# A hybrid decoder layer on one core: fewer hand-overs inside the samples' attention, two background tasks issued later, another warm-up

## The chip, the cores and the metric

The kernel runs on one core of a Trainium2 chip. The core has five engines that work side by side, each through its own queue in order: TensorE (PE, matrix products; the loading of its weights is shown apart as PEld), VectorE (DVE), ScalarE (ACT), GpSimd (POOL) and SyncE (SP), which here only issues transfers. Matrix products read SBUF and write PSUM, eight banks of 128 partitions x 512 floats. Transfers from HBM run on 16 shared DMA engines, whichever queue issued them.

The metric is the device time of one launch, in microseconds (us). Before the change the median of three runs is 2834.9 us (2831.94 to 2835.55).

## The reference, cut to what matters

One decoder layer is computed for two groups that share all weights: a prompt of 256 tokens and 8 samples of 8 new tokens each, with 2048 tokens in the past. That gives 320 columns in all.

```python
x = layer_norm(ALPHA * x + 0.5 * swiglu(x, ffn1_w_up, ffn1_w_down))        # 2048 -> 2 x 5632 -> 2048
rq, rk, rv, rg, nq, nkv, ng = split(x @ w_in)                              # one input projection
ro = silu(rg) * group_norm(retention(rope(rq), rope(rk), rv, state))       # 4 heads
# NSA, 8 query heads, 2 KV heads, three branches:
kc, vc = compress(k_cmp), compress(v_cmp)                                  # blocks of 32 keys, stride 16
p_cmp  = softmax(q @ kc);  o_cmp = p_cmp @ vc
idx    = top_k(p_cmp @ cover, 16)                                          # 16 blocks of 64 keys
o_slc  = softmax(q @ k_slc[idx]) @ v_slc[idx]
o_win  = softmax(q @ k_win) @ v_win                                        # last 512 keys
no     = g0 * o_cmp + g1 * o_slc + g2 * o_win
x = layer_norm(ALPHA * x + concat(ro, no) @ w_out)
x = layer_norm(ALPHA * x + 0.5 * swiglu(x, ffn2_w_up, ffn2_w_down))        # then the outputs
```

All arithmetic is float32 in name. The kernel splits each weight and each activation into a high and a low part of a shorter float format (`fp32r`) and adds three products: high x high, high x low, low x high (`mm3`, L213 to L217).

## The kernel before

**Main products.** All weight matrices are cut into chunks of 512 KB (256 rows x 512 columns) which pass in one fixed order through four raw buffers, three split buffers and four PSUM banks `m0` to `m3`. A chunk is loaded by an SP transfer (`w_load`, L269), split by ACT (high part, L221) and DVE (low part, L222), and used in 4 x 6 = 24 products of 128x128 weights by 320 columns (`sweep`, L301). `w_feed` (L275) issues splits and loads at each new chunk; a load waits on the SP queue until the split of the chunk that held its raw buffer is done.

**Background tasks.** Everything else (compression, selection, the samples' attention, the prompt's attention, retention, the norms' small work) is written as Python generators, and the program's order is fixed when it is built, by a planner. The planner has a clock, the sum of the nominal PE times of all products issued so far. After every six main products, nominally 0.816 us, `main` calls `tick` (L231), which advances up to two tasks that are due. A task says with `yield t` that it wants to go on t us of the planner's clock later, and with `yield condition` that it waits for a condition. A `yield 0.0` also ends the task's step: it goes on at the next tick at the earliest, after six more main products. `until` (L248) advances tasks without main products until a condition holds. The clock is an estimate; on the chip every engine follows the fixed order and waits by semaphores.

**Samples' attention** (`sample`, L1289). It takes four groups of two samples, one after the other. Each group reads ten tiles: the window keys (`wkt`), four tiles of paged keys (`pks`, 8 transfers of 128 KB each on SP, after two loads of page numbers), the window values (`cwin`), four tiles of paged values (`pvs`, two gathers each on POOL, L1223). The tiles share a ring of slots: two at first, four once the selection of all groups is done (`a_count == 4`), three after `r1` is taken away (L1480). `feed` (L1299) keeps the ring full less one and estimates when each tile arrives: 2.5 us after the issue or the previous tile's estimate, whichever is later, plus 4.5 us for paged keys and 3.0 us for others. `arrival()` is what is left of that estimate, zero if it is past. Keys: scores of one tile (`coltile`, eight PE records), then 0.7 us later scaling and the block mask on DVE, then the next tile. Values: `turn(c)` transposes four pieces of the probabilities on PE (L1377) and copies them out on DVE or ACT; `values(c)` multiplies them with the tile (32 PE records). Tile c's `values` comes after `turn(c+1)`.

**Selection** (`select`, L1229). For each of the four groups: scores of compressed keys, softmax, scaling by the reciprocal (L1247, DVE), a pause of 1.5, transposition (L1250, PE), then ranking of 30 blocks by five DVE passes over 900 elements. After group g it sets `a_count = g + 1`. `sample` starts group g when `a_count > g`. After the fourth, `v_natural` (L1103) transposes the prompt's values in three steps and then sets `vn_done`, for which `prompt` (L1543) waits; `mix` (L1516) waits for the last sample group and the last prompt head and starts retention. The evacuation of the retention queries (L1447) runs tasks until `a_count == 4`, and the second half of the output projection (L1938) runs tasks until retention is done.

**Prompt's compression** (`prompt_compress`, L1124). Sixteen weight tiles of 512 KB (`cw1k`, `cw1v`) pass through two halves of a buffer. The first two are loaded at the start of the task; each of the others is issued on SP when the tile two places before it is used. The products start 7.0 us after the task begins, one tile every 2.8 us. `pc_done` at its end is awaited by `select`.

**Start** (L322). While the first inputs come in, PE multiplies a matrix of constants by itself 11 times (float32, 128 columns, L347; each product leaves two records) into a bank that is not read.

Of the kernel before, what the change touches and what calls it, by code (L numbers as in the profile page):

```python
# [9 lines left out]
F32R = mybir.dt.float32r  # L10
# [13 lines left out]
SCALE = 128.0 ** -0.5  # L24
PAST = 2048

WARM = 11
NTMP = 5


# [139 lines left out]
class Builder:  # L170
# [38 lines left out]
    def mm(self, out, lhsT, rhs, start, stop, us):  # L209
        self.nc.tensor.matmul(out, lhsT, rhs, start=start, stop=stop)  # L210
        self.clock += us
# [110 lines left out]
    def start(self):  # L322

        self.x_rings = [self.sb.ring(4 * KT * NT, name=f"x{k}") for k in range(2)]

        self.kh, self.kl = 0, 1
        self.xh, self.xl = ([self.x_room(k, [128, NT], F32R) for _ in range(KT)] for k in range(2))
        raw = [self.t([128, 6, NT], f"G{5 + i}") for i in range(3)]
        self.xraw = [raw[q // 3][:, 2 * (q % 3):2 * (q % 3) + 2] for q in range(8)]
        for q in range(8):  # L330
            if q:
                self.nc.sync.dma_start(out=self.xraw[q], in_=self.I["xT"][:, 2 * q:2 * q + 2, :])
            else:

                r, w = self.raw[:, 0], self.wq[0]
                self.nc.sync.dma_start(out=self.xraw[0], in_=self.I["xT"][:, 0:2, :])
                for k in range(2):
                    self.nc.sync.dma_start(out=r[:, 512 * k:512 * k + 512], in_=w[:, 512 * k:512 * k + 512])
                self.raws[0], self.n_dma = r, 1
            if 0 < q < 4:  # L340
                self.w_load()

        self.ones = self.t([128, 128], "ones")
        self.nc.vector.memset(self.ones, 1.0 / 256.0)
        ps = self.p("m3")
        for _ in range(WARM):
            self.nc.tensor.matmul(ps[:, 0:128], self.ones, self.ones, start=True, stop=True)  # L347
        hi, lo = (self.t([128, 1024], t, F32R) for t in ("wh0", "wl0"))
        r = self.raws.pop(0)
        for k in range(2):  # L350
            c = slice(512 * k, 512 * k + 512)
            self.split(self.xh[k], self.xl[k], self.xraw[0][:, k])
            self.split(hi[:, c], lo[:, c], r[:, c])
        self.halves[0] = hi, lo
        self.n_split = 1
        self.x_split(1)
        self.w_split()
# [766 lines left out]
    def prompt_compress(self):  # L1124
        nc = self.nc
        wk = self.vn[:, 1536:1920]
        stage = self.t([128, 2, 1024], "G6")

        def load(n):
            raw = stage[:, n % 2]  # L1130
            nc.sync.dma_start(out=raw, in_=self.I["cw1" + "kv"[n // 8]][n % 8])
            return raw

        raws = [load(0), load(1)]
        yield 7.0
        for kind in range(2):
            ph = yield from self.hold()
            for i in range(8):
                raw = raws.pop(0)
                for s2 in range(2):  # L1140
                    s = 2 * i + s2
                    for r in range(2):
                        j = (2 * s + r) % 4
                        o = (s2 * 2 + r) * 256

                        at = 640 * kind + 16 * r + s
                        self.mm(ph[32 * j:32 * j + 32, 0:256], self.kvt[:, at:at + 497:16],
                                raw[:, o:o + 256], s < 2, s >= 14, 0.127)
                if 8 * kind + i < 14:
                    raws.append(load(8 * kind + i + 2))  # L1150
                yield 2.8
            h4 = wk[:, 0:256]
            nc.scalar.activation(h4, ph[:, 0:256], AF.Copy)
            self.drop(ph)
            yield 1.0
            pf = yield from self.hold()
            for f in range(2):
                self.mm(pf[:, 32 * f:32 * f + 32], h4[:, 128 * f:128 * f + 128], self.k_sum4, True, True, 0.43)
            hs, u = wk[:, 256:320], wk[:, 320:384]
            for f in range(2):  # L1160
                pc = self.posc[:, 2 * kind + f:2 * kind + f + 1]
                nc.scalar.activation(hs[:, 32 * f:32 * f + 32], pf[:, 32 * f:32 * f + 32], AF.Identity, bias=pc)
                nc.scalar.activation(u[:, 32 * f:32 * f + 32], pf[:, 32 * f:32 * f + 32], AF.Square, bias=pc)
            self.drop(pf)
            yield from self.gelu(hs, u)
            yield 3.0
            po = yield from self.hold()
            w2 = self.cw2[kind]
            if kind == 0:
                for f in range(2):  # L1170
                    self.mm(po[:, 0:32], w2[:, f], u[:, 32 * f:32 * f + 32], f == 0, f == 1, 0.43)
                for v in range(2):
                    nc.scalar.activation(self.kcp(v), po[:, 0:32], AF.Copy, scale=0.5)
            else:
                for f in range(2):
                    self.mm(po[0:32, 0:128], u[:, 32 * f:32 * f + 32], w2[:, f], f == 0, f == 1, 0.22)
                nc.scalar.activation(self.vcp[0:32], po[0:32, 0:128], AF.Copy, scale=0.5)
            self.drop(po)
            yield 1.0
        self.pc_done = True  # L1180
# [48 lines left out]
    def select(self):  # L1229
# [7 lines left out]
        for g in range(4):  # L1237
# [7 lines left out]
            self.drop(px)  # L1245
            yield from self.softmax(s, sc, None, (0.8, 0.8))
            nc.vector.tensor_scalar(s, s, sc[:, 0:1], None, op0=ALU.mult)  # L1247
            yield 1.5
            px = yield from self.hold()
            nc.tensor.transpose(px[:, :128], s, self.ident)  # L1250
            self.clock += 0.11
# [37 lines left out]
    def sample(self):  # L1289
# [9 lines left out]
        def feed():  # L1299
            while len(kvq) < len(self.ring) - 1 and order:  # L1300
                g, i = order.pop(0)
                self.kv_time = max(self.kv_time, self.clock + 2.5) + (4.5 if 0 < i < 5 else 3.0)
                kvq.append((self.kv_load(g, i), self.kv_time))

        def arrival():
            return max(0.0, kvq[0][1] - self.clock)

        def take():
            self.kv_tags.pop(0)
            return kvq.pop(0)[0]  # L1310
# [4 lines left out]
        for g in range(4):  # L1315
# [5 lines left out]
            pnn, o = ptr[:, 1536:1664], ptr[:, 1664:1792]  # L1321
# [14 lines left out]
            def new_rows(keys, dst):  # L1336
                pn = yield from self.hold()
                self.coltile(pn, slice(0, 16), q, lambda b, v: keys(v)[:, gs], True, True, 0.07)
                add(dst, pn[:, 0:16], SCALE, self.k_mn, op0=ALU.mult, op1=ALU.add)
                self.drop(pn)  # L1340


            for c in range(4):
                yield arrival()
                kt = take()
                px = yield from self.hold()
                self.coltile(px, slice(0, 512), q, lambda b, v: kt[:, b, :, 128 * v:128 * v + 128], True, True, 0.234)
                feed()
                if c == 1 and g:
                    yield from new_rows(self.kw, sw[:, 512:528])  # L1350
                if c == 2 and g:
                    yield from self.softmax(sw[:, :528], scw, self.grow[:, g, 2:3], (0.8, 0.8))
                yield 0.7
                add(s[:, 512 * c:512 * c + 512].rearrange("p (k r) -> p k r", r=64),
                    px.rearrange("p (k r) -> p k r", r=64), SCALE,
                    self.bm[:, g, 8 * c:8 * c + 8].rearrange("p (k o) -> p k o", o=1).broadcast_to([128, 8, 64]),
                    op0=ALU.mult, op1=ALU.add)
                self.drop(px)
# [28 lines left out]
            def values(c, vt):  # L1387
                n, pt = 1 if c == 5 else 4, pts.pop(c)
                at = 128 * ((c + 3) // 4)
                for k in range(n):  # L1390
                    rhs = (lambda b, v: self.vnew[:, v]) if c == 5 else (lambda b, v: vt[:, b, k, 128 * v:128 * v + 128])
                    self.coltile(po, slice(at, at + 128), lambda j: pt[:, 128 * k + 32 * j:128 * k + 32 * j + 32],
                                 rhs, c in (0, 1, 5) and k == 0, c in (0, 4, 5) and k == n - 1, 0.081)
# [4 lines left out]
            nc.gpsimd.memset(pnn, 0.0)  # L1398
            nc.gpsimd.tensor_scalar(pnn[:, 16 * g:16 * g + 16], s[:, 2048:2064], scs[:, 0:1], None, op0=ALU.mult)
            nc.gpsimd.tensor_scalar(pnn[:, 64 + 16 * g:80 + 16 * g], sw[:, 512:528], scw[:, 0:1], None, op0=ALU.mult)  # L1400
            yield 1.0
            yield arrival()
            values(0, take())
            feed()
            yield 3.5
# [1 line left out]
            yield 1.2  # L1407
            for c in range(1, 5):
                yield from turn(c + 1)
                yield arrival()  # L1410
                values(c, take())
                feed()
                if c < 4:
                    yield 1.8
# [564 lines left out]
```

## Time and profile before

| | |
|---|---|
| median of 3 runs | 2834.9 us |
| the profiled execution, its own time | 2837.03 us |
| its span, first to last instruction | 2835.4 us |
| mean granted TensorE clock | 0.994 |
| PE busy | 2778.3 us, 98% |
| DVE, ACT, POOL busy | 1553.6, 1212.1, 335.4 us |
| HBM read, written | 467.47 MB, 22.28 MB |

Times below are us from the span's start. PE's idle time is the difference between a stretch's length and PE's busy time in it. "Waits" list who waited for whom: us in total, times, longest. A timeline row gives start, length, engine, line, operation, output tile and input tiles, with the idle time before it and what ended it in brackets. `m` tiles are main products, `x` tiles are products of background tasks. "PEclk" is the granted share of the TensorE clock.

### The profile page before, as it was taken

Reading aid. Unit: us, or ns where it says so; the run is one execution under the profiler, and the core shown is the slowest. Engines: PE = TensorE matmul, PEld = TensorE weight load, DVE = VectorE, ACT = ScalarE, POOL = GpSimd, SP = SyncE. Lnnn points to the kernel's source line nnn. Section 1 sums busy time; section 2 is a strip of 40 time slices with the busy share of each in tenths; the row PEclk is TensorE's granted clock in tenths of the full one; section 3 lists DMA queues with packets and bytes.
Section 4 is the critical chain, followed back from the end, with each engine's and each line's share of the span. In section 5 each row is a group of like instructions: output and inputs, shape, how many; then the busy total and the mean of one; then the engine's idle time right before and its main releaser. Section 6 shows DMA issues by size and latency. Waiting matters only on the chain. (4 is left out here: it accounts for less than half of the span.)

```text
span 2835.4 us, 49605 instructions
## 1 busy us (share of the span) xinstructions
PE 2778.3 (98%) x19839; PEld 2704.3 (95%) x19839; DVE 1553.6 (55%) x1933; ACT 1212.1 (43%) x1677; POOL 335.4 (12%) x398
## 2 busy tenths in 40 slices
PE   9999999999999999999999999999999999999997
PEld 9999999999999989998888888999999999999997
DVE  4333333347867769783574455674333333367665
ACT  4333333345445546554444445353333333354554
POOL 0000000000113223213232111330000000001110
PEclk9999999999999999999999999999999999999999
DMA  6555444455656445447667764545444444444442
GB/s 230 182 192 181 149 149 149 151 161 193 202 169 227 144 137 157 141 138 254 200 235 236 234 212 161 207 140 165 150 149 149 150 150 152 151 143 148 150 150 101
DMA packets 201594, 484.75 MB, mean 171 GB/s; under 512 B 24146, under 2 KB 98771, under 8 KB 199443
## 3 DMA queue, kind: packets, MB, share of 16 engines
q1 hardware_dynamic: 191538, 451.30, 49.9%
q0 software_dynamic: 9824, 30.29, 3.1%
q8 instruction: 155, 2.54, 0.4%
q14 instruction: 77, 0.62, 0.1%
HBM read 467.47 MB, written 22.28 MB: 173 GB/s over the span
## 5 line engine op out<-in xcount | busy, mean ns | idle before, releaser
L222 DVE TENSOR_TENSOR wl<-raw,wh 128x1024 fp32r<-128x1024 f32 (+1 forms) x651 | 815.6, 1253 | 1067.3 <-ACT wh L221 1054.5
L221 ACT ACTIVATE wh<-raw 128x1024 fp32r<-128x1024 f32 (+1 forms) x651 | 688.1, 1058 | 1164.8 <-PE m L216 1125.8
L215 PE MATMUL m<-x,wh 128*128 128x320 f32 x3664 | 1144.4, 312 | 3.3 <-ACT x L617 1.5
L216 PE MATMUL m<-x,wh 128*128 128x320 f32 x3664 | 1128.5, 308 | 1.7 <-DVE x L597 1.0
L217 PE MATMUL m<-x,wl 128*128 128x320 f32 x3664 | 1128.5, 308 | 0.2 <-DVE wl L222 0.2
L215 PEld LDWEIGHTS m<-x,wh 128*128 128x128 f32 x3664 | 688.1, 188 | 26.7 <-issue 22.2
L216 PEld LDWEIGHTS m<-x,wh 128*128 128x128 f32 x3664 | 688.4, 188 | 2.8 <-DVE x L597 1.3
L217 PEld LDWEIGHTS m<-x,wl 128*128 128x128 f32 x3664 | 687.7, 188 | 0.8 <-DVE wl L222 0.7
L215 PE MATMUL m<-r,wh 128*128 128x320 f32 (+1 forms) x1592 | 495.2, 311 | 4.0 <-ACT r L221 2.3
L216 PE MATMUL m<-r,wh 128*128 128x320 f32 (+1 forms) x1592 | 488.2, 307 | 4.4 <-DVE r L222 4.4
L217 PE MATMUL m<-r,wl 128*128 128x320 f32 (+1 forms) x1592 | 490.8, 308 | 0.0
L215 PEld LDWEIGHTS m<-r,wh 128*128 128x128 f32 x1592 | 298.9, 188 | 9.9 <-issue 3.7
L216 PEld LDWEIGHTS m<-r,wh 128*128 128x128 f32 x1592 | 299.6, 188 | 6.6 <-DVE r L222 5.8
L217 PEld LDWEIGHTS m<-r,wl 128*128 128x128 f32 x1592 | 298.3, 187 | 0.0
L518 POOL TENSOR_TENSOR t<-x 128x320 f32<-128x320 f32 x3 | 2.8, 919 | 1418.5 <-DVE x L498 716.6
L222 DVE TENSOR_TENSOR r<-G,r 128x640 fp32r<-128x640 f32 (+1 forms) x184 | 155.5, 849 | 0.0
L215 PE MATMUL x<-r,G 128*128 128x256 f32 x480 | 137.6, 287 | 0.0
L216 PE MATMUL x<-r,G 128*128 128x256 f32 x480 | 135.7, 283 | 0.0
L217 PE MATMUL x<-r,G 128*128 128x256 f32 x480 | 135.1, 282 | 0.0
L221 ACT ACTIVATE r<-G 128x640 fp32r<-128x640 f32 (+1 forms) x184 | 130.1, 712 | 0.0
L222 DVE TENSOR_TENSOR r<-x,r 128x512 fp32r<-128x512 f32 (+1 forms) x76 | 79.5, 1053 | 35.9 <-ACT r L221 34.6
L215 PEld LDWEIGHTS x<-r,G 128*128 128x128 f32 x480 | 91.8, 191 | 1.0 <-issue 1.0
(394 smaller groups left out, 2233.1 us busy)
## 6 DMA issues: line engine op xcount, KB each, us to landing
raw<-wup SPq DMA_DIRECT2D x351, 512.0 KB, 3.5
raw<-wdn SPq DMA_DIRECT2D x176, 512.0 KB, 3.6
raw<-win_ret SPq DMA_DIRECT2D x48, 512.0 KB, 4.3
raw<-win_nsa SPq DMA_DIRECT2D x40, 512.0 KB, 3.8
raw<-wout SPq DMA_DIRECT2D x32, 512.0 KB, 3.7
r<-pks SPq DMA_DIRECT2D x96, 128.0 KB, 3.5
x<-pkc SPq DMA_DIRECT2D x152, 64.0 KB, 2.3
K<-cw1k SPq DMA_DIRECT2D x16, 512.0 KB, 4.5
```

The lines of the kernel that those rows point to most:

```text
L215: mm(out, wh, xh, start=start, stop=False)
L216: mm(out, wh, xl, start=False, stop=False)
L217: mm(out, wl, xh, start=False, stop=stop)
L221: self.nc.scalar.activation(hi, src, AF.Copy)
L222: self.nc.vector.tensor_tensor(lo, src, hi.bitcast(F32), op=ALU.subtract)
L518: nc.gpsimd.tensor_tensor(s, self.d[0], self.d[1], op=ALU.add)
```

## The change

Five edits of the planned order, none of the computation:

- the warm-up is 24 products of an `fp32r` copy of the constants, 160 columns each, with two alternating 128-column weights, instead of 11 float32 products; a DVE copy of 128x512 makes their operand first
- the prompt's compression starts its products 9.0 instead of 7.0 after its first loads
- the selection's transposes come 2.8 instead of 1.5 after the scaling
- before a paged key tile, and before the value tiles 1 to 4, the task hands over only if `arrival()` is not zero; a zero no longer ends the step
- before value tile 0 the two pauses, 1.0 and then `arrival()`, become one pause of the larger of the two, taken at the earlier moment

The `yield arrival()` before the window keys (L1325) stays.

```diff
-WARM = 11
+WARM = 24
...
-        for _ in range(WARM):
-            self.nc.tensor.matmul(ps[:, 0:128], self.ones, self.ones, start=True, stop=True)
+        warm = self.t([128, 1024], "wh2", F32R)[:, 0:512]
+        self.nc.vector.tensor_copy(warm.rearrange("p (k c) -> p k c", k=4),
+                                   self.ones.rearrange("p (o c) -> p o c", o=1).broadcast_to([128, 4, 128]))
+        for k in range(WARM):
+            self.nc.tensor.matmul(ps[:, 0:160], warm[:, 128 * (k % 2):128 * (k % 2) + 128], warm[:, 256:416], start=True, stop=True)
...
         raws = [load(0), load(1)]
-        yield 7.0
+        yield 9.0
...
             nc.vector.tensor_scalar(s, s, sc[:, 0:1], None, op0=ALU.mult)
-            yield 1.5
+            yield 2.8
             px = yield from self.hold()
             nc.tensor.transpose(px[:, :128], s, self.ident)
...
             for c in range(4):
-                yield arrival()
+                if arrival():
+                    yield arrival()
                 kt = take()
...
-            yield 1.0
-            yield arrival()
+            yield max(1.0, arrival())
             values(0, take())
...
             for c in range(1, 5):
                 yield from turn(c + 1)
-                yield arrival()
+                if arrival():
+                    yield arrival()
                 values(c, take())
```

## The prediction

> **What bounds the kernel now.** First the page, then PE's time by stretches, then PE's waits.
>
> ```profile
> span 2835.4 us, 49605 instructions
> PE 2778.3 (98%) x19839; PEld 2704.3 (95%) x19839; DVE 1553.6 (55%) x1933; ACT 1212.1 (43%) x1677; POOL 335.4 (12%) x398
> 10.40:20.00 9.60, 9.60 (x66) 9.60 (x67) 5.96 (x9) 6.20 (x12) 0.00 (x0) 1.00 0.99 392
> 1310.00:1380.00 70.00, 70.00 (x517) 62.92 (x515) 26.35 (x35) 29.83 (x52) 19.97 (x33) 1.00 0.66 217
> sum 420.00, PE 405.50 PEld 356.87 DVE 224.20 ACT 181.82 POOL 94.31; mean PE 57.93 PEld 50.98 DVE 32.03 ACT 25.97 POOL 13.47
> PE x L210 <- DMA K<-pvs,vrow: 3.3, 1, 3.3
> PE x L1250 <- DVE G L1247: 3.0, 2, 1.8
> PE x L210 <- DMA r<-pks: 2.5, 2, 1.3
> PE x L210 <- DMA G<-cw1k: 2.1, 1, 2.1
> PE m L215 <- ACT wh L221: 1.0, 1, 1.0
> PE x L210 <- DMA K<-pks: 0.7, 1, 0.7
> ```
>
> PE is busy 98% of the span, so the kernel is as long as PE's work plus PE's waits. Main products run 66 in 9.60 us (the third row, busy counts in brackets), 0.145 us each, six of them in 0.87 us. The sum row covers 1290 to 1710, the stage of the attention: 420.0 - 405.5 = 14.5 us idle. That is all that reordering there can win besides the cost of changing between products of different tasks. Of it, 5.1 us (3.0 + 2.1) are waits that two edits address by name, and 6.5 us (3.3 + 2.5 + 0.7) are waits for key and value tiles.
>
> **Compression 2.0 later.**
>
> ```profile
> 1288.82 1.21 PE L210 MATMUL x<-cw2v,r 128*128 128x128 f32 x8
> 1293.17 0.54 POOL L948 DMA_DIRECT2D K<-c_aside  x1
> 1293.57 0.38 SPq L1131 DMA_DIRECT2D G<-cw1k  x1
> 1303.39 0.68 PE L210 MATMUL x<-G,G 128*32 128x256 f32 x8 [2.07 <-DMA G<-cw1k]
> ```
>
> The fourth tile was issued at 1293.57 while a 1 MB reload (`c_aside`, 1293.17) shared the DMA engines, and PE wanted it at 1303.39 - 2.07 = 1301.32. A pause of 9.0 instead of 7.0 is two or three turns of six main products; the other task's products at 1288.82 also move the planner's clock, so I take some 1.9 us of later use (its 0.97 until the next main products, one turn of 0.9). The load itself is issued later too, but it stands behind a weight load on SP, in a stretch where the queue is behind anyway. Bounds: 0 (the landing moves as much) to -2.1; I take **-1.9**, nearer to the row. All of selection follows `pc_done` and moves about 2 us later against the main products.
>
> **Selection's transposes.**
>
> ```profile
> 1402.49 0.33 PE L1250 MATMUL x<-ident,G 128*128 128x128 f32 x1 [1.26 <-DVE G L1247]
> 1441.54 1.22 DVE L222 TENSOR_TENSOR wl<-raw,wh 128x1024 fp32r<-128x1024 f32 x1 [1.51 <-PE m L217]
> 1442.87 0.29 DVE L1247 TENSOR_SCALAR G<-G,sc 128x128 f32<-128x128 f32 x1
> 1443.31 0.30 PE L1250 MATMUL x<-ident,G 128*128 128x128 f32 x1 [1.77 <-DVE G L1247]
> ```
>
> Two of four transposes waited for the scaling, which stood on DVE behind a split. 1.3 more of planner time is one or two turns, 0.9 to 1.8 us of main products in PE's queue, against waits of 1.26 and 1.77. Bounds: -1.2 to **-3.0**, and I take the latter, since two turns are the commoner case (2.8 / 0.816 rounds up to 4, 1.5 / 0.816 to 2). Four groups together end 4 to 8 turns later, so `a_count == 4`, the prompt's attention and then retention start later by roughly 6 to 9 us of main work. What hides that is the length of the projection itself. If the cover is gone, the end of retention is late: PE already waited 1.0 there (the row `ACT wh L221`). Bounds -1.0 to +3; I take 0, because the prompt's chain is stepped by the same two-per-tick limit that the removed hand-overs used up.
>
> **Hand-overs before value tiles.**
>
> ```profile
> 1483.21 0.61 PE L1377 MATMUL x<-ident,r 128*128 128x128 f32 x4
> 1483.58 0.40 PE L215 MATMUL m<-x,wh 128*128 128x320 f32 x1
> 1484.63 1.08 PE L210 MATMUL x<-r,G 128*32 128x128 f32 x32
> 1485.64 0.41 PE L215 MATMUL m<-x,wh 128*128 128x320 f32 x1
> ```
>
> Between `turn` and `values` stand six main products, from 1483.58 to 1484.63, 1.05 us, where 0.87 is their time in a long run. Without the hand-over the twelve products around it are one run, and one such break, 0.18 less some 0.05 between two background pieces, goes. 4 tiles x 4 groups x 0.13 = **-2.0** (bounds -1.0 to -2.9). The copies that `values` needs are made one `turn` earlier, so they are no new wait.
>
> The other side: each tile is wanted a turn earlier. In the first group the gathers stand behind the softmax on POOL:
>
> ```profile
> 1462.29 0.32 POOL L1400 TENSOR_SCALAR G<-ln,sc 128x16 f32<-128x16 f32 x1
> 1464.14 1.64 POOL L1223 DMA_INDIRECT K<-pvs,vrow  x1 [0.30 <-DMA raw<-win_ret]
> 1468.63 0.41 PE L210 MATMUL x<-K,G 128*32 128x128 f32 x4
> 1472.33 1.25 PE L210 MATMUL x<-K,G 128*32 128x128 f32 x28 [3.29 <-DMA K<-pvs,vrow]
> ```
>
> The gather cannot start before L1400 is done, whatever PE does, and PE waited 3.29 for it. Value tile 0 comes one turn earlier and tile 1 another, so up to two turns, 2 x 0.95, of cover turn into wait: **+1.9** (bounds 0, if the whole group shifts with its softmax, to +3.5, if the ropes of the retention queries get ahead of the gathers on POOL). Queued behind this wait on PE are the main products, nothing else.
>
> ```profile
> 1473.10:1476.40 3.30, 3.30 (x19) 2.92 (x14) 1.21 (x2) 2.05 (x7) 3.14 (x4) 0.50 0.75 303
> ```
>
> After that wait the granted clock (third last column) was 0.50 for 3.3 us: about 1.5 us lost, which the run before pays already. The shorter wait of 1.29 below left it at 1.00. By the rule of the Trainium skill, page "TensorE: Matmul & The Clock Gate", section "HAM oscillation — how this bites in real kernels", an idle gap above some 3.4 us sends PE back to half clock; by it three longer key waits would cost 1.5 us each and the sum would come out 4.5 higher, by the rows seen so far nothing. I leave it out of the sum.
>
> **Hand-overs before key tiles.** Here the scaling of the tile before has no PE work, so no break is saved; the key tile only comes a turn earlier.
>
> ```profile
> 1637.50 5.06 SPq L684 DMA_DIRECT2D K<-pks  x8
> 1643.63 4.30 SPq L684 DMA_DIRECT2D r<-pks  x8
> 1650.84 1.05 PE L210 MATMUL x<-r,G 128*32 128x512 f32 x4
> 1653.18 1.05 PE L210 MATMUL x<-r,G 128*32 128x512 f32 x4 [1.29 <-DMA r<-pks]
> 1583.12 1.05 PE L210 MATMUL x<-K,G 128*32 128x512 f32 x4 [0.69 <-DMA K<-pks]
> ```
>
> SP needs 4 to 5 us to issue one tile (8 transfers) and a weight load stands between two of them, so tiles come some 6 us apart (1637.50, 1643.63), while the planner reckons 4.5. The last tile of a group is late already: from 1650.84 to 1653.18 the first half's 1.05 and a wait. In the first group the ring has two slots and the estimate is always ahead (2.5 + 4.5 = 7.0), nothing changes. In the third and fourth, adding up the nominal times between the tiles, the estimates are ahead for the first three tiles, and only the last has its estimate behind it: one turn, 0.95, of cover becomes wait in each. In the second, with four slots, the tiles come about two turns earlier in all, one of which the slack hides. 3 x 0.95 = **+2.9** (bounds 0, if SP gets to the tiles earlier too, to 3 groups x 4 tiles x 0.95 = +11.4).
>
> **Warm-up.**
>
> ```profile
> 0.98 0.17 DVE L344 MEMSET ones<- 128x128 f32 x1 [0.98 <-PEq L1973]
> 5.22 0.69 DVE L222 TENSOR_TENSOR wl<-raw,wh 128x512 fp32r<-128x512 f32 x1 [0.31 <-ACT wh L221]
> 5.20:5.70 0.50, 0.50 (x6) 0.50 (x5) 0.47 (x1) 0.50 (x2) 0.00 (x0) 1.00 1.01 273
> ```
>
> The copy takes at most the 0.69 of a split of its size, so PE starts about 0.7 later than before, near 1.9. Six records in 0.50 us near 5.4 show that PE was already fast by then. 24 products of 160 columns at half clock take 160/320 x 2 x 0.145 = 0.145 each, 3.5 us, and end near 5.4, as now. The next thing that PE waits for is the first low part, done at 5.22 + 0.69 = 5.91, so earlier is worth nothing: **0** (bounds -0.2 to +0.6, if it ends later or the clock rises later). The same page of the Trainium skill, section "Part 1: The HAM clock gate (the "warmup" mystery)", says that the gate looks at windows of 3.4 us that run freely, not at a count of products; by it a start 0.7 later shifts the fast clock by nothing or by a whole window, by the row's alignment nothing. No run here shows the other.
>
> **Sum.** -1.9 - 3.0 - 2.0 + 1.9 + 2.9 + 0 = -2.1. The profiled run took 2837.03 with a span of 2835.4, 1.6 outside; it becomes 2834.9. It lies 2.1 above the median of the runs, 2834.9, from which I count: **2832.8 us**.
>
> **The rivals.**
>
> *Earlier use frees slots earlier* (faster). A tile's transfer may start when its slot's last reader is done. If attention runs ahead as a whole, the loads run ahead with it and the waits for tiles stay as they are; then -1.9 - 3.0 - 2.0 remain, and the 1.0 at the end of retention may go: 2834.9 - 7.9 = 2827.0. For it: the tile rows show waits of only 0.69 and 1.29 with PE as the last reader. Against it: SP's issues follow one another without a gap.
>
> *SP is the bound of the key phases* (slower). In the last three groups SP issues tiles back to back, and every turn of main products taken out of the key phase is PE standing still instead. With +11.4 for the keys, +1.9 for the gather and one more stretch at half clock, +1.5: 14.8 - 6.9 = +7.9, 2842.8 us. It decides from the point where more than 6.9 / 0.95 = 7 of the hand-overs' turns are uncovered, and shows as slower from 13 on (6.9 + 5.7 over 0.95). For it: the 6 us spacing of the issues against 4.5 planned. Against: the estimates hold most key tiles back.
>
> *The edit does little* (the change does not do what it says). If `arrival()` is rarely zero, only the two pauses act: -4.9 and half of the breaks, -1.0, less the gather's 1.9: 2834.9 - 4.0 = 2830.9.
>
> **How the numbers follow.** 0.2% is 5.7 us, about what a measurement of this kernel can tell from no change: faster is below 2829.2, slower above 2840.6. Forecast 0.35, earlier slots 0.31, SP bound 0.23, little effect 0.11. The forecast's own range is 2829 to 2838, and little effect lies in it; a small part of both, 0.02, falls below 2829.2. Faster 0.33, same 0.44, slower 0.23. The range reaches to both outer cases, where half of each is left out at most: 2825 to 2843.
>
> **What would show it.** Right: no wait on L1247 or `cw1k`; `values` directly after L1377; PE idle from 1290 to 1710 between 10 and 15 us; the wait for `pvs` near 5. Wrong: waits for `pks` above 5 us in total, or more stretches with a clock of 0.50 after 1380 (SP bound); tile waits as before (earlier slots); or a wait near 1790 that has grown beyond 1.0, by which the later prompt would be the cause.

## The result, and the profile after

The changed kernel is slower: 2866.05 us, median of four runs (2864.24 to 2869.35), against 2835.23 for the kernel before on the same chip. The ratio is 1.0108 with a 95% interval of 1.0095 to 1.0122. Below, ratios are turned into microseconds as (ratio - 1) x 2835, so the change is +30.6 (+26.9 to +34.6). The profiled execution took 2866.43.

The page of after, its span and the busy time of its engines:

```profile
span 2864.8 us, 49601 instructions
PE 2789.9 (97%) x19841; PEld 2710.2 (95%) x19841; DVE 1553.5 (54%) x1934; ACT 1212.3 (42%) x1677; POOL 332.8 (12%) x398
```

The span grew by 29.4 us. PE's busy time grew by 11.6 (2778.3 to 2789.9), although the same products are computed save two more warm-up records; its idle time grew by 17.8 (57.1 to 74.9). Both need an explanation, and the forecast had only looked at idle time.

PE's windows of before, then of after (us, PE busy with its count, PEld, DVE, ACT, POOL, granted clock, DMA share, GB/s):

```profile
1450.00:1530.00 80.00, 75.86 (x651) 66.26 (x652) 47.97 (x83) 36.68 (x76) 30.00 (x31) 0.98 0.72 243
1530.00:1610.00 80.00, 78.67 (x721) 69.06 (x712) 40.01 (x82) 31.94 (x75) 14.83 (x18) 1.00 0.72 231
1690.00:1770.00 80.00, 79.32 (x597) 71.53 (x597) 43.97 (x76) 41.01 (x82) 9.11 (x15) 1.00 0.44 155
1770.00:1850.00 80.00, 78.98 (x502) 76.04 (x501) 54.95 (x75) 27.95 (x38) 32.73 (x26) 1.00 0.54 189
```

```profile
1450.00:1530.00 80.00, 67.72 (x568) 55.82 (x568) 39.63 (x69) 27.16 (x63) 19.38 (x23) 0.94 0.68 230
1530.00:1610.00 80.00, 73.62 (x616) 62.81 (x615) 41.42 (x81) 35.04 (x75) 16.77 (x19) 0.98 0.61 198
1690.00:1770.00 80.00, 74.11 (x572) 66.97 (x574) 38.55 (x81) 39.23 (x97) 5.92 (x11) 1.00 0.44 153
1770.00:1850.00 80.00, 74.36 (x489) 70.04 (x490) 47.27 (x64) 32.41 (x47) 26.21 (x19) 0.98 0.44 158
1290.00:1710.00 420.00, 395.62 (x3248) 342.60 (x3247) 210.88 (x354) 167.16 (x336) 88.60 (x117) 0.98 0.67 222
```

Two places lose. From 1450 to 1610 the idle time rose from 5.5 to 18.7 us, with the clock down to 0.94; from 1690 to 1850 it rose from 1.7 to 11.5. The last row is the stretch of the forecast: 420.0 - 395.6 = 24.4 us idle, where 10 to 15 was foretold.

What PE waited for in after (us in total, times, longest):

```profile
PE x L210 <- DMA r<-pks: 10.2, 5, 5.0
PE m L215 <- DVE x L1937: 5.6, 2, 3.4
PE m L215 <- DVE K L961: 5.1, 2, 2.7
PE x L1610 <- DVE G L1601: 4.5, 7, 2.2
PE x L210 <- DMA r<-pvs,vrow: 4.2, 2, 3.2
PE x L210 <- DVE G L1614: 1.5, 1, 1.5
```

The two waits that the change addressed are gone: no row names the scaling or `cw1k`. In their place stand waits for key tiles (the same row was 2.5 before), for the ropes of the retention queries and keys (L961), for the prompt's softmax (L1601) and for the evacuations of the output projection (L1937, the line L1933 of before; of the last three, before had only 1.7 for the softmax).

Where the time sits on PE, and the stretches at half clock that follow:

```profile
1465.38 0.41 PE L215 MATMUL m<-x,wh 128*128 128x320 f32 x1 [2.35 <-DVE K L961]
1473.37 0.87 PE L210 MATMUL x<-r,G 128*32 128x128 f32 x12 [3.24 <-DMA r<-pvs,vrow]
1519.38 1.80 PE L210 MATMUL x<-r,G 128*32 128x512 f32 x4 [5.02 <-DMA r<-pks]
1533.08 0.55 PE L215 MATMUL m<-x,wh 128*128 128x320 f32 x1 [2.75 <-DVE K L961]
```

```profile
1471.76:1478.59 6.83, 5.22 (x41) 4.72 (x42) 0.14 (x1) 0.00 (x0) 5.61 (x8) 0.50 0.35 110
1519.55:1522.96 3.41, 3.20 (x8) 0.22 (x4) 0.00 (x0) 0.00 (x0) 0.00 (x0) 0.50 1.06 370
1533.20:1536.61 3.41, 3.41 (x13) 3.41 (x14) 2.53 (x6) 3.34 (x5) 3.25 (x5) 0.50 0.51 154
1816.51:1819.92 3.41, 3.41 (x14) 3.41 (x15) 1.70 (x2) 0.57 (x2) 2.42 (x2) 0.50 0.20 38
sum 30.70, PE 27.83 PEld 22.30 DVE 16.59 ACT 13.55 POOL 13.98; mean PE 3.48 PEld 2.79 DVE 2.07 ACT 1.69 POOL 1.75
```

Each of the three longest waits shown has such a stretch beginning in it or just behind it, and so has one of 3.44 for an evacuation, which ends at 1816.35. The sum is that of all eight stretches between the start and the last products, of which four are shown; before it was 20.47 in five. At half clock the main products follow one another every 0.267 us (13 steps from 7.21 to 10.68 at the start, two rows of which are shown below) instead of every 0.145, so some 45% of a stretch is lost, and 10.2 us more of it are an estimated 4.7 us of busy time. That is a balance: behind 1290 after has 20.5 us at half clock against 3.4, and ahead of it, in stages whose order is the same, 10.2 against 17.1.

The start shows the rest of that kind:

```profile
1.66 5.41 PE L350 MATMUL m<-wh 128*128 128x160 f32 x24 [1.66 <-DVE wh L347]
6.86 0.55 PE L215 MATMUL m<-x,wh 128*128 128x320 f32 x1
7.21 0.47 PE L216 MATMUL m<-x,wh 128*128 128x320 f32 x1
7.48 0.47 PE L217 MATMUL m<-x,wl 128*128 128x320 f32 x1
10.91 0.31 PE L215 MATMUL m<-x,wh 128*128 128x320 f32 x1
```

The 24 products follow one another every 0.21 us, the first main product comes at 6.86 (5.64 before), and PE got its full clock only near 10.9 (5.35 before). From 11 on the same main product starts 2.1 us later than in before; 0.25 of that is idle time, 1.8 is busy time. With 4.7 that explains 6.5 of the 11.6; the rest of it I did not find.

### The profile page after: what moved, and what is told of

It reads as the page before. It is cut to its first block, busy times and chain, and to the rows that moved or that the text cites. A ratio compares the mean times of both kernels' runs of the same rounds, so it can differ in the third digit from the quotient of the medians.

```text
span 2864.8 us, 49601 instructions
## 1 busy us (share of the span) xinstructions
PE 2789.9 (97%) x19841; PEld 2710.2 (95%) x19841; DVE 1553.5 (54%) x1934; ACT 1212.3 (42%) x1677; POOL 332.8 (12%) x398
## 5 line engine op out<-in xcount | busy, mean ns | idle before, releaser
L215 PEld LDWEIGHTS m<-x,wh 128*128 128x128 f32 x3664 | 689.1, 188 | 30.6 <-issue 20.0
```

The source lines that it names most:

```text
L215: mm(out, wh, xh, start=start, stop=False)
```

## The experiments

Four theories. **T1**: the later selection and compression push the chain selection, prompt, retention past the ends of the projections, where the plan runs them without main products or lets them collide with the sweeps' own work. **T2**: the removed hand-overs turn cover into waits for tiles. **T3**: the warm-up costs 2 us. **T4**, formed after the first round: any other order costs, wherever it differs.

### One edit at a time

Handed over less (the three edits of the samples' attention), selection, compression, warm-up, each alone on the kernel before:

```diff
 e1 (key tiles; value tiles 1 to 4 alike)
-                yield arrival()
+                if arrival():
+                    yield arrival()
 e1 (value tile 0)
-            yield 1.0
-            yield arrival()
+            yield max(1.0, arrival())
 e2
-            yield 1.5
+            yield 2.8
 e3
-        yield 7.0
+        yield 9.0
 e4
-WARM = 11
+WARM = 24
...
-            self.nc.tensor.matmul(ps[:, 0:128], self.ones, self.ones, start=True, stop=True)
...
+            self.nc.tensor.matmul(ps[:, 0:160], warm[:, 128 * (k % 2):128 * (k % 2) + 128], warm[:, 256:416], start=True, stop=True)
```

> Before with the three hand-over edits of the samples' attention alone. Theory 1 (the later selection and compression cost the time, by pushing the prompt's chain past the ends of the sweeps): -3 to +4 us against before, waits for pks tiles below 6 us in total, no new stretch at clock 0.50 after 1500. Theory 2 (the removed hand-overs turn cover into waits for key and value tiles): +12 us or more, waits for pks near 10 and for pvs near 5, two or more half-clock stretches more than before after 1400. Theory 3 (the warm-up): no difference.

> Before with the selection's pause of 2.8 instead of 1.5 alone. Theory 1: +8 to +20 us, with the waits on the ropes of L961 above 5 us, and waits on L1937 near 1780 to 1800 above 3 us. Theory 2: -3 to 0 us, the waits on L1247 gone and nothing in their place. Theory 3: no difference.

> Before with the compression's pause of 9.0 instead of 7.0 alone. Theory 1: +2 to +8 us, since all of selection is some 8 main products later and the prompt's chain ends later by as much; the wait on cw1k (2.1) gone. Theory 2: -2 us, the wait gone and nothing in its place. Theory 3: no difference.

> Before with the new warm-up alone. Theory 3: +2 us from the start (24 products of 0.21 us end near 6.9 instead of 5.6, and the clock rises near 10.7), carried unchanged to the end, and every row after 20 as before. Theories 1 and 2 take the same +2 for this part, no more; if the start shifts where later half-clock stretches fall, up to 1.7 us more or less for each.

| kernel | ratio to before | 95% interval | us |
|---|---|---|---|
| e1, hand-overs | 1.0045 | 1.0029 to 1.0062 | +12.8 |
| e2, selection | 1.0081 | 1.0063 to 1.0099 | +23.0 |
| e3, compression | 1.0038 | 1.0024 to 1.0052 | +10.8 |
| e4, warm-up | 1.0000 | 0.9989 to 1.0011 | 0.0 |

The selection is the largest, above T1's +8 to +20, and the compression is above T1's +2 to +8, though both intervals reach into the ranges; the hand-overs fit T2's time but not its waits (4.4 and 1.3 for key tiles, not 10). The warm-up's 2 us lies inside its interval of 3 either way. Alone, the edits sum to 46.6, half as much again as the change, so some of their cost is shared.

What the selection's pause did when it came alone:

```profile
PE m L215 <- DVE x L1933: 4.9, 2, 2.8
PE x L210 <- DMA K<-pvs,vrow: 4.9, 2, 4.4
PE x L210 <- DMA K<-pks: 3.5, 1, 3.5
PE x L1427 <- DVE G L1423: 3.2, 1, 3.2
```

The two waits on the scaling, 3.0 together, are gone. In their place four rows are new or larger, up to 400 us later. L1427 is the last samples' group, which the plan now forces before the last gates of the projection (`until` at L1473): nothing covers the additions that join its three branches (L1423).

Where the loss falls shows when the starts of the same main product are compared with those in the profile of before. The projection is the stretch from 1280 to 1713 there, the output projection's part with retention that from 1713 to 1803; at both ends the kernels have done the same background work, but for at most 12 of 1589 products. The first of the two numbers varies: kernels whose plan is the same nearly up to 1713 (after and e13, e3 and e16, e8 and e14) differ by 0.4 to 4.0.

| kernel | later by, projection, us | later by, output projection, us |
|---|---|---|
| after | 21.3 | 7.8 |
| e1, hand-overs | 11.1 | -0.1 |
| e2, selection | 17.9 | 6.5 |
| e3, compression | 3.8 | 9.2 |
| e4, warm-up | -0.8 | 0.0 |

### After, with one thing put back or made room for

```diff
 e5, on after (and e10, e12 below):
     def main(self, gen):
         for _ in gen:
-            self.tick()
+            self.tick(3 if self.a_count == 4 and not self.mixed else 2)
 e6, on after:
-            yield 2.8
+            yield 1.5
```

> After, with up to three tasks instead of two advanced per turn from the fourth selection group on until the prompt's attention is mixed. In the planned order this ends the prompt's chain and the samples' groups 12 main products (of 128 weights, in threes) earlier, ahead of the projection's end instead of forced behind it; every edit stays. Theory 1 (the chain pushed past the projection's end costs the time there): 10 to 16 us below after, that is +13 to +21 against before, the waits at 1705 to 1735 and on L1937 after 1770 gone, those near 1462 to 1475 staying. Theory 2 (the hand-overs' waits for tiles cost it): within 4 us of after. Theory 4 (the order of before was tuned, and any other order costs some 10 us by new collisions, wherever it differs): anywhere from +20 to +40 against before.

> After, with the selection's pause back at 1.5. In the planned order nothing is then forced: the fourth selection group ends 12 products ahead of the retention queries, the prompt's chain 10 ahead of the projection's end, which the removed hand-overs make room for. Theory 1: +3 to +10 us against before, since the later compression alone no longer passes the end. If each edit costs its own sum, wherever the end is: +22 (12 of the hand-overs, 10 of the compression). Theory 2: +12 or more, by waits for pks and pvs of 8 us or more in total.

e5 is at 1.0059 (1.0038 to 1.0080), +16.7, 13.9 below after; the waits at 1705 to 1735 shrank to one of 2.9, and those on L1937 to 0.6. That is T1's number, but only in part T1's place: in the profiles the loss in the output projection is gone (7.8 to -0.1), that in the projection hardly changed (21.3 to 18.4). e6 is at 1.0041 (1.0024 to 1.0058), +11.6: the selection accounts for 19.0 of after's 30.6, give or take some 6, since each of the two is known to 4 or 5. By the profiles the loss in the projection is 9.3 with the old pause instead of 21.3, that in the output projection 4.2 instead of 7.8. Its +11.6 is a little above T1's +3 to +10 and well below the +22 of edits that each cost their own: with the hand-overs gone there is room in the plan, and the later compression costs nothing that shows on top of e1's +12.8.

### The other direction, and two halves of the hand-overs

```diff
 e7
-            yield 1.5
+            yield 0.7
 e8 (before value tiles 1 to 4; value tile 0 as in e1) and e15 (before key tiles alone)
-                yield arrival()
+                if arrival():
+                    yield arrival()
 e11 (before key tiles and value tiles 1 to 4; value tile 0 as in e1 where g > 0)
-                yield arrival()
+                if g == 0 or arrival():
+                    yield arrival()
```

> Before, with the selection's pause at 0.7, one turn earlier instead of two later. In the planned order the samples' groups and the prompt's chain end at the same products as before. Theory 1: 0 to +4 us, four waits on L1247 of about 1.8 each instead of two (3.0 in total), nothing behind 1480. Theory 4: +8 us or more, from waits at other places.

> Before, with the hand-over edits at the value tiles alone, those at the key tiles as before. The forecast's terms for it were -2.0 and +1.9, so 0; the terms for the key tiles +2.9. If the value tiles carry the cost that the three edits showed together (+12): +8 to +14, with a wait for pvs of 4.8 and more and half-clock stretches behind it. If the key tiles carry it: -2 to +3, waits for pks below 3 us.

> Before, with the hand-over edit at the key tiles alone. In the planned order retention ends 6 products later than before, with its reciprocals 12 and 8 ahead of the evacuations, as where 3.4 us of waits were seen. The forecast's term is +2.9 for three tiles a turn earlier; the bound +11.4 for all of them. If position and those three tiles are all: +5 to +9, waits for pks of 2 to 5 us. If the issue of the key tiles on SP bounds the phases: +12 or more, waits for pks above 8.

> Before, with the hand-over edits in the second to fourth group of samples only. Theory 2, in the form that the gather of the first group carries the cost: the wait for pvs back at some 3.3 and one half-clock stretch of 3.4 behind it instead of 6.8, so 3 to 4 us less than with all groups (+12): +8; if the key tiles of the later groups carry it: +10 to +14; if the end of the prompt's chain carries it (its end is planned at the same product as before): 0 to +4.

| kernel | ratio | 95% interval | us |
|---|---|---|---|
| e7, selection a turn earlier | 1.0037 | 1.0026 to 1.0048 | +10.5 |
| e8, value tiles | 1.0061 | 1.0038 to 1.0084 | +17.3 |
| e15, key tiles | 1.0040 | 1.0026 to 1.0054 | +11.3 |
| e11, groups 2 to 4 | 1.0028 | 1.0019 to 1.0038 | +7.9 |

e7 has T4's time at T1's place, and shows what a wait really costs. A row of its list of waits, the two transposes, and the sum of its half-clock stretches between 1390 and 1530:

```profile
PE x L1250 <- DVE G L1247: 7.7, 2, 4.8
```

```profile
1397.99 0.43 PE L1250 MATMUL x<-ident,G 128*128 128x128 f32 x1 [2.90 <-DVE G L1247]
1437.20 0.45 PE L1250 MATMUL x<-ident,G 128*128 128x128 f32 x1 [4.79 <-DVE G L1247]
```

```profile
sum 17.06, PE 15.50 PEld 13.26 DVE 7.33 ACT 6.20 POOL 3.25; mean PE 3.88 PEld 3.31 DVE 1.83 ACT 1.55 POOL 0.81
```

Before had 3.41 us at half clock there. The page of e7 has 6.7 us more busy time than before; 17.06 - 3.41 = 13.65 us more at half clock are some 6.2 of it. Its idle time is 0.3 less (56.8), though the waits on L1247 grew from 3.0 to 7.7: a wait near 1020, ahead of the edit, was 1.8 here and 5.5 in before. Of the 17.06, 10.24 belong to the two waits shown, some 4.7 us of lost time. So the longer waits cost twice, 4.7 us as idle time and about as much again as half clock.

e8 and e15 each cost about as much as all three edits together; the intervals of the three overlap. In e8 the wait for the gather (`pvs`) is 5.3 instead of 3.3, as forecast (+1.9), with 6.8 us at half clock behind it instead of 3.4. By the starts of the same main products e8 loses 10.6 us in the projection and 11.2 in the output projection, so about half of its cost falls behind the attention; e15 loses 7.6 and 4.1. e15 waited 2.7 for `r<-pks`, 3.0 for the evacuation of a gate (L1475) and 3.4 for those of the output projection. e11 is 5 below e1, about as much as their intervals can tell apart; all of its loss lies in the projection (8.3 and 0.0). Its interval, +5.4 to +10.8, holds the case of the gather (+8), touches that of the later groups' key tiles and leaves out that of the chain's end (0 to +4).

### Retention's place in the sweep

In e2, e3, e8 and after PE waited at two points of the output projection. VectorE there in e8, whose next PE row is `1774.59`, and then in e14, where retention starts later:

```profile
1766.85 2.15 DVE L1747 RECIPROCAL G<-G 128x320 f32<-128x320 f32 x1
1769.84 2.15 DVE L1747 RECIPROCAL G<-G 128x320 f32<-128x320 f32 x1
1772.83 1.22 DVE L222 TENSOR_TENSOR wl<-raw,wh 128x1024 fp32r<-128x1024 f32 x1
1773.96 1.68 DVE L1933 TENSOR_TENSOR x<-x,m 128x320 f32<-128x320 f32 x4
...
1774.59 0.61 PE L215 MATMUL m<-r,wh 128*128 128x320 f32 x1 [2.83 <-DVE x L1933]
```

```profile
1763.36 0.48 DVE L1933 TENSOR_TENSOR x<-x,m 128x320 f32<-128x320 f32 x1
...
1770.48 2.15 DVE L1747 RECIPROCAL G<-G 128x320 f32<-128x320 f32 x1
1773.48 2.14 DVE L1747 RECIPROCAL G<-G 128x320 f32<-128x320 f32 x1
```

The group norm of two heads takes 6 us on DVE (two reciprocals of 2.15, their products). If it comes up when a sweep ends, the four evacuations queue behind it, and the next sweep needs their banks. In e14 it comes up after them, and nothing waits for them. Four runs move retention alone, one repeats the compression with three tasks per turn, and one is its control:

```diff
 e9, on before; e13, on after, with 5.0; e14, on e8, with 8.2; e16, on e3, with 6.5
-        self.spawn(self.k_natural())
+        self.spawn(self.k_natural(), 2.5)
 e12, on before; e10, on e3
-            self.tick()
+            self.tick(3 if self.a_count == 4 and not self.mixed else 2)
```

> Before, with the task that transposes retention's keys (and all of retention behind it) starting 2.5 later in the planner's time; nothing before 1715 differs. In the planned order retention ends 6 products (in threes) later. Theory 1, in the sharper form that the runs so far suggest (the group norm's two pairs of reciprocals on DVE, 6 us each, fall just ahead of the evacuations that end a sweep of the output projection; the kernels with retention 6 or more products later show 3.4 to 5.6 us of waits there and half-clock stretches, the others at most 1.0): +4 to +9 us, waits for DVE's evacuations of the output projection of 3 us or more in total. Theories 2 and 4 as told: 0 for the one; for the other +10 at places that differ from these.

> After, with the transposition of retention's keys, and retention behind it, starting 5.0 later still. In the planned order the reciprocals of the two pairs of heads then stand 4 and 8 products behind the evacuations of their sweeps, instead of 2 ahead of the one and in the midst of the other. If position costs the time: waits on L1937 between 1770 and 1830 from 5.6 us to below 2, a half-clock stretch of 3.4 gone, 4 to 9 us below after, that is +22 to +27 against before. If lateness costs it: 3 us or more above after.

> Before, with the hand-over edits at the value tiles (as measured, +17 to +20, with 5.5 us of waits on L1933 and 10.2 us at half clock in the last stretch) and retention 8.2 later. In the planned order the reciprocals stand 6 to 10 products behind the evacuations instead of 4 to 8 ahead. If position costs the time: 8 to 11 us less, that is +7 to +11 against before. If lateness: +20 or more.

> Before, with the compression's pause of 9.0 and retention 6.5 later. In the planned order the reciprocals stand 2 to 6 products behind the evacuations instead of 2 to 6 ahead. If position costs the time: 6 to 9 us less than with the later compression alone (+10.5), that is +1 to +5 against before. If lateness: +12 or more.

> Before, with the compression's pause of 9.0 and up to three tasks per turn from the fourth selection group until the prompt's attention is mixed. In the planned order retention starts 4 products later than before instead of 12. Theory 1: the tail's loss of the compression edit (waits of 6.5 and some 13.7 us at half clock behind 1700) goes, its gain ahead of 1450 stays: -6 to +2 against before. Theory 4: +8 or more.

> Before, with up to three tasks per turn in the same stretch and nothing else: the control of the runs with three. In the planned order the prompt's chain ends at the same product. Theory 1: -2 to +3. Theory 4: +8 or more.

| kernel | ratio | 95% interval | us | without the move |
|---|---|---|---|---|
| e9 | 1.0014 | 1.0005 to 1.0024 | +4.0 | 0 |
| e13 | 1.0077 | 1.0060 to 1.0094 | +21.8 | +30.6 |
| e14 | 1.0051 | 1.0034 to 1.0068 | +14.5 | +17.3 |
| e16 | 1.0021 | 1.0011 to 1.0030 | +6.0 | +10.8 |
| e10 | 1.0008 | 0.9998 to 1.0018 | +2.3 | +10.8 |
| e12 | 1.0033 | 1.0019 to 1.0048 | +9.4 | 0 |

The waits for these evacuations follow one number of the planned order: how many main products (groups of three) the reciprocals of the first and the second pair of heads stand ahead of the first evacuation of their sweep, or behind the last.

| kernel | reciprocals | waits for L1933 or L1937, us | later by, output projection, us |
|---|---|---|---|
| before | 18 and 14 ahead | none | 0 |
| e1, e5, e10 | 14 and 10 ahead | 0.6, 0.6, 0.6 | -0.1, -0.1, -0.1 |
| e6, e9, e15 | 12 and 8 ahead | 3.4, 3.4, 3.4 | 4.2, 2.6, 4.1 |
| e8 | 8 and 4 ahead | 5.5 | 11.2 |
| e2, e3 | 6 and 2 ahead | 4.9, 4.9 | 6.5, 9.2 |
| after | 2 ahead, amid the second | 5.6 | 7.8 |
| e16 | 2 and 6 behind | 0.5 | 1.4 |
| e13, e14 | 4 to 10 behind | none, none | 0.9, 6.6 |

So the position costs, not the lateness: moved past the evacuations the later retention is nearly free of these waits in all three kernels, and all three lie below what lateness was expected to cost. In time the move won 8.8 of after's 30.6 (4 to 9 expected), 4.8 of e3's (6 to 9 expected) and 2.8 of e8's (8 to 11 expected); by their intervals these differences are known to some 6, 5 and 8, so in time only the first is clear. By the profiles e13 and e16 lose 0.9 and 1.4 in the output projection instead of 7.8 and 9.2. In e14 it is 6.6 instead of 11.2, with a wait for a split (`wh`, 2.7 us) in their place. One execution of each kernel is profiled, and that of e14, with 2845.77, is 6.8 below its median.

e10 fits T1: the later compression, with its chain brought forward, costs 2.3 (-0.6 to +5.1) instead of 10.8. But the control contradicts T1. With three tasks per turn and no edit, the plan ends where it did, and the kernel is 9.4 slower, by waits that were not there before:

```profile
1600.86 0.30 PE L1606 MATMUL x<-ident,G 128*128 128x128 f32 x1 [3.93 <-DVE G L1597]
...
1628.07 0.69 PE L1509 MATMUL x<-ident,t 128*128 128x128 f32 x3 [2.92 <-ACT t L1467]
```

Each has a stretch of 3.4 us at half clock behind it. So T4 holds too: e7 and e12 leave the plan's ends where they were, e15 moves them by 6 products, and all three still cost 9 to 11. No kernel of the sixteen is below before; only e4 and e10 have an interval that holds 1.

## Why the prediction was wrong

The forecast was 2832.8 in a range of 2825 to 2843, with 0.23 for slower. It came out 23 above the range.

- **Compression, -1.9.** The wait went, as said. That all of selection "moves about 2 us later against the main products" was right and priced at nothing: alone it cost +10.8, most of it where retention now met the evacuations (9.2 of the 13.0 by which its main products came later; waits of 4.9, and 10.2 us at half clock from 1765 to 1800) and where the last samples' group was forced (2.6).
- **Selection, -3.0, and nothing downstream.** This is the step that failed. The waits on the scaling went, and the chain behind `a_count == 4` cost +23.0 alone and 19 of the 30.6 within after. I had named the end of the chain and put -1.0 to +3 on it, because the prompt "is stepped by the same two-per-tick limit". The plan says otherwise: before, the fourth group ended 16 main products (again in threes) ahead of the retention queries that need it, and the prompt's chain 16 ahead of the projection's end. The change used up both, and there `until` runs them bare. In the trace of after these two places show as a wait of 2.4 us right behind the queries (1465.38) and as 4.0 us of waits for the prompt's last heads at the projection's end (1725 to 1731). That is 6.4 us of the 19; by the profiles some 12 of it lie in the projection and some 4 in the output projection, where retention came later. The later `a_count == 4` also holds back loads, because the ring has four slots only from then on: SP issued the second group's first key tile at 1488.8 in after and 1490.8 in e2, against 1482.3 in before and 1477.7 in e6. How the rest of the 12 divides between key tiles, gather and other places was not measured.
- **Value tiles, -2.0.** The saving does not exist. The row that I read, 1.05 us between `turn` and `values` for six main products, held the tail of the transposes. In after the same work without the main products between:

```profile
1487.16 0.61 PE L1381 MATMUL x<-ident,r 128*128 128x128 f32 x4
1487.70 1.08 PE L210 MATMUL x<-r,G 128*32 128x128 f32 x32
1488.71 0.41 PE L215 MATMUL m<-x,wh 128*128 128x320 f32 x1
```

From `turn` to the next main product: 1488.71 - 1487.16 = 1.55. Before: 1485.64 - 1483.21 = 2.43, less six main products of 0.145, again 1.56. The other value tiles with nothing else between, four of before and seven of after, give 1.54 to 1.57 in the same way. This change between tasks costs PE nothing here.
- **The gather, +1.9.** The wait grew from 3.3 to 5.3 in e8, as foretold (4.2 in after, with the later selection). Its half clock doubled from 3.4 to 6.8 us, some 1.6 of lost time more, which the sum left out.
- **Key tiles, +2.9.** The mechanism was there, its size was not: the row `r<-pks` grew by 7.7 us, from 2.5 to 10.2, in after, though only to 2.7 in e15. The bound of the SP rival, +11.4, comes nearer. Ahead of the longest of these waits (5.0, at 1519.38) SP issued tile after tile with one weight load between, as that rival has it:

```profile
1495.52 11.38 SPq L687 DMA_DIRECT2D r<-pks  x16
1507.97 5.74 SPq L687 DMA_DIRECT2D r<-pks  x8
```

But SP alone is not the cause, since putting back the selection's pause brought the row to 3.8 (e6). Together the three hand-over terms were +2.8; alone the hand-overs measured +12.8.
- **Half clock, left out.** It was weighed at 4.5 us and set aside, "by the rows seen so far nothing". Behind 1290 after has 17.1 us more of it, some 7.8 of busy time. The Trainium skill, page "TensorE: Matmul & The Clock Gate", section "HAM oscillation — how this bites in real kernels", gives as a rule no idle gaps of PE above some 3.4 us. The traces side with the rule's direction, but shorter gaps than that were enough here (last section).
- **Warm-up, 0.** Not contradicted in time (1.0000, to 3 us either way), wrong in its working: 24 products took 5.2 us, not 3.5, the copy 0.43, and the first main product came at 6.86 instead of 5.64. After ran 2.1 us behind by 20, the profiled e4 1.5; the interval is too wide to show it, so that the time fits is no proof of the working.

What would show it right or wrong had been listed: the waits on L1247 and `cw1k` gone and `values` directly behind L1377 came true; idle time of 10 to 15, a `pvs` wait near 5 did not (24.4 and 4.2), and of the signs of "wrong" three appeared: waits for `pks` above 5, more stretches at half clock, and the grown wait near 1790 "by which the later prompt would be the cause". The rival that ended slower had the direction, and the key phases do hold the largest row of waits in after. But it priced only the hand-overs, and the largest part came from the term that I had costed at nothing.

What stays open: of the 11.6 of e6 the profile puts about a third in the output projection, with retention's place, but the rest is not split between key waits, the gather and their half clock, and the runs cannot say why so many neighbours of this order cost about 10, only that each shows new waits of some 1.5 to 5 us, many of them for DVE or ACT.

## What to carry to other kernels

In a kernel whose order is fixed when it is built, price a delay at the end of its chain too, not only at the wait that it removes: read from the plan how many products lie between each step and the point that needs it, and do not put a margin that the delay eats at nothing. A margin that is kept is no guarantee (e7, e12). Ask of every long instruction on a side engine what stands right behind it in that queue; the position of 6 us of VectorE work against the banks' evacuations went with 3 to 11 us of the output projection here. And count a wait of 3 us on PE as some 4.5, for the half clock that mostly followed it in this kernel.

## What the runs showed that was not expected

**How short a wait brings half clock.** In the 18 profiles, of PE's waits between 1290 and 1950, all 23 above 3.1 us had a stretch at half clock beginning during them or within 3.5 us after, 11 of 13 from 2.8 to 3.1, 16 of 26 from 2.2 to 2.8, and 29 of 78 from 1.3 to 2.2, some of these from a longer wait nearby. The granted stretches are 3.41 us or 6.83. So a wait well below 3.4 us can suffice.

**The new warm-up did not bring the clock up.** With the old products full clock came between 4.2 and 7.3 us from the start (13 profiles), with the new ones between 8.7 and 11.3 (5 profiles), although they keep PE's rows filled from 1.66 on; that is 1.8 to 4.4 us after the first main product at 6.9. Whether their type, their width or their alternating weights is the cause was not tried.

**Reciprocals.** One of 128x320 on VectorE took 2.15 us, against 0.48 for an addition of that shape.
